# When the modulation blocks are multiplied, and where the decays' logarithms stand

## The chip, the cores and the metric

The kernel runs on one core of one Trainium2 chip. The metric is the device time of one execution in microseconds (us): lower is better. TensorE is called PE, VectorE DVE, ScalarE ACT, GpSimd POOL and SyncE SP; SP issues most of the transfers (DMA).

## The reference, cut to what matters

Two layers of a diffusion backbone over 512 latent tokens and 256 context tokens, width 1024. The first layer is a bidirectional retention with 4 heads, the second a gated MLP. Ahead of each layer the normed tokens are scaled and shifted by vectors that come from a conditioning vector (the modulation):

```python
shift_x, scale_x, gate_x = jnp.split(silu_c @ ada_w[i] + ada_b[i], 3, axis=-1)
shift_c, scale_c, gate_c = jnp.split(silu_cc @ ada_w[i] + ada_b[i], 3, axis=-1)
hx = rmsnorm(x, norm_g[i]) * (1 + scale_x[:, None]) + shift_x[:, None]
hc = rmsnorm(ctx, norm_g[i]) * (1 + scale_c) + shift_c
...
log_g = jax.nn.log_sigmoid(decay_logit.astype(F32))
...
q = to_heads(h @ w_in[:, :a], RET_HEADS)
k = to_heads(h @ w_in[:, a:bq], RET_HEADS) * (RET_QK_DIM ** -0.5)
v = to_heads(h @ w_in[:, bq:cq], RET_HEADS)
z = h @ w_in[:, cq:]
```

`log_g`, eight numbers (four heads, two directions), enters the retention as exponents of the decay between tokens.

## The kernel before, in words

The large products are done in single precision by splitting each operand into a high and a low part: three products (low by high, high by low, high by high) in place of one (`mm3`). ACT copies the high part and DVE subtracts it to get the low part (`split`, tiles `hl`). The token-times-weight products are further arranged as fast 2x2 block products with seven in place of eight (`Product`, with the names B11, T1, T2, B21, T3, B22, T4); the sums of blocks that this needs are formed by DVE, of the weights in the tiles `raw`, of the tokens in `oS1` to `oS4`, and of the results in the tiles `snap`. In a product 24 PE instructions belong to one step.

The first projection (`kq` of head 0) is plain, because its tokens are only just being made. It runs over eight blocks of 128 features, `kb` = 0 to 7; we call them steps. For each block:

- `ada0_mm(kb, ...)` multiplies the conditioning vector by the block's modulation weights (tile `ada_w`), 16 PE instructions per block, into one PSUM bank; ACT copies the bank to a tile `adae`.
- `ada0_cols(kb, es, n)` turns this by transposes, two per block, and four small DVE operations make the scale `gs0` and the shift `sh0` of the block, or of two blocks (n = 2).
- `come(...)` applies scale and shift to the block's tokens (DVE, ACT, DVE) and leaves the high and low part in tiles `oA..` and `oS..` (latent) or `hc` (context).
- `plain(kb, th, ...)` does the products of the block.

The context tokens come later: their two halves are loaded to `cq[0]` and `cq[1]`, transposed for their norms in `half_rows` after step 3, and `spread(2)` with the copy to `rs2` makes their norm factors after step 4. They enter in steps 4 to 6 (`CTX_COME`) and are multiplied in steps 5 to 7 (`CTX_PLAIN`).

Behind the first projection comes a pair of `vz` quads (values and gates of head 0, `PAIRED`), whose products alternate between the two quads, and then nine single quads (`SINGLE`), n = 0 to 8. Each is a stretch of about 24 us on PE. `decay_logs` makes `lg` from the eight logits in ten DVE operations and two of ACT (Exp and Ln) on tiles of 8 columns; before, it is called in the paired quads, after product B22 of the first quad. `lg` is first read by `decay(0)`, during n = 5.

What sets the order: each engine runs its instructions in the order in which they stand in its queue. Up to the end of the first projection this is the order of the text, for PE throughout. After that (`act.kept = dve.kept = False`) the instructions of ACT and DVE are put in order when the kernel is compiled, by what is ready, near the order of the text. SP issues loads in the order of the text; the weights `raw` go through a queue `Q` of loads and splits, and `Q.get()` hands out a split weight and sees that the next two are split as well. Small products of `ones` (`between_modes`) are put at chosen places in the stream of PE.

Of the kernel before, what the change touches and what calls it, by code (L numbers as in the profile page):

```python
# [67 lines left out]
def hybrid_kernel(ctx, tc, xT_d, cT_d, cv_d, sv_d, rows_d, ada0_d, adag_d, w_d, rope_d, dec_d, ws_d, id_d, out_d):  # L68
# [13 lines left out]
    def st(shape, tag, dt=F32, bufs=1, name=None):  # L82
        return sb.tile(shape, dt, tag=tag, name=name or tag, bufs=bufs)

    T2 = 11
# [32 lines left out]
    def t2(name, shape=(P, 512), dt=F32):  # L118
        return st(list(shape), "t2", dt, bufs=T2, name=name)

    def pt(shape=(P, 512), tag="ps"):
        return ps.tile(list(shape), F32, tag=tag, name="pst", bufs=6 if tag == "ps" else 2)
# [208 lines left out]
    def op(key):  # L331
        A[key] = st([P, 2, 4, HS], "o" + key, F32R)
# [12 lines left out]
    def features(bank, a, w, fresh, ks=range(4)):  # L345

        for kt in ks:
            if kt == 3 and inside:
                inside.pop(0)()
            r = (a[:, 0, kt, :], a[:, 1, kt, :])  # L350
            for s in range(2):
                o = s * 512 + kt * P
                mm3(bank[:, s * HS:s * HS + HS], (w[:, 0, o:o + P], w[:, 1, o:o + P]), r, fresh and kt == 0 and s == 0, kt == 3)
# [143 lines left out]
    def decay_logs():  # L497
        la = st([P, 8], "la")
        lb = st([P, 8], "lb")
        lc = st([P, 8], "lc")  # L500
        dve.tensor_scalar(la, dlog, -1.0, None, ALU.mult)
        dve.tensor_tensor(la, la, dlog, ALU.min)
        act.activation(la, la, AF.Exp)
        dve.tensor_scalar(lb, la, 1.0, None, ALU.add)
        act.activation(lg, lb, AF.Ln)
        dve.tensor_scalar(lc, lb, -1.0, None, ALU.add)
        dve.tensor_tensor(lc, la, lc, ALU.subtract)
        dve.reciprocal(lb, lb)
        dve.tensor_tensor(lc, lc, lb, ALU.mult)
        dve.tensor_tensor(lg, lg, lc, ALU.add)  # L510
        dve.tensor_scalar(la, dlog, 0.0, None, ALU.min)
        dve.tensor_tensor(lg, la, lg, ALU.subtract)
# [9 lines left out]
    def half_rows(at, g, t, tag="ps"):  # L522

        for i in range(2):
            pq = pt(tag=tag)
            for k in range(4):
                pe.transpose(pq[:, k * P:k * P + P], at(k)[:, i * P:i * P + P], ident)
            if i == 0:
                act.activation(t2("junk0"), pq, AF.Square, scale=1.0 / 32.0, accum_out=sq[t][:, g, 0:1])
            else:  # L530
                dve.bn_stats(bnx[:, t, g, :], pq)
# [23 lines left out]
    def ada0_mm(*kbs, then=None):  # L555

        n = len(kbs)
        pa = pt((P, HS * n), tag="tm")
        for i, kb in enumerate(kbs):
            rows = ada_w.pop(kb)  # L560
            for k in range(KT):
                j = k % 4
                mm(pa[32 * j:32 * j + 32, i * HS:i * HS + HS], cpad[:, k, :], rows[k // 4][:, j * HS:j * HS + HS],
                   start=(k < 4 and i == 0), stop=(k >= 4), skip_group_check=True)
        if then:
            then()
        e = t2("adae", (P, HS * n))
        act.copy(e, pa)
        return e

    def ada0_cols(k0, e, n=1):
        pq = pt((P, HS * n), tag="tm")
        for b in range(2 * n):
            pe.transpose(pq[:, b * P:b * P + P], e[:, b * P:b * P + P], ident)
        s = st([P, 2 * n, 2], "ada_s" if n == 1 else "ada_s2", bufs=2, name="ada_s")
        v = pq.rearrange("p (c g r) -> p c r g", c=2 * n, g=4)
        dve.tensor_reduce(s, v[:, :, 0:2, :], axis=AX.X, op=ALU.add)
        ss = s.rearrange("p (n b) r -> p n b r", b=2)
        ks = slice(k0, k0 + n)
        dve.tensor_tensor(gs0[:, ks, :], ss[:, :, 0, :], adab0[:, 1, ks, :], ALU.add)  # L580
        dve.tensor_tensor(sh0[:, ks, :], ss[:, :, 1, :], adab0[:, 0, ks, :], ALU.add)
        dve.scalar_tensor_tensor(gs0[:, ks, :], gs0[:, ks, :], 1.0, g0[:, ks, :], ALU.add, ALU.mult)
# [67 lines left out]
    def come(*what, then=None):  # L650


        made = []
        for kb, th in what:
            g, k = divmod(kb, 4)
            r = th // 2
            if r:
                f, h, l = cq[g][:, k, :], hc[:, 0, kb, :], hc[:, 1, kb, :]
            else:
                name = NAMES[th][g]  # L660
                if k == 0:
                    A[name] = st([P, 2, 4, HS], AT_S3.get(name, "o" + name), F32R)
                f, h, l = xk(th, g, k), A[name][:, 0, k, :], A[name][:, 1, k, :]
            dve.scalar_tensor_tensor(f, f, gs0[:, kb, r:r + 1], rs[th], ALU.mult, ALU.mult)
            made.append((f, sh0[:, kb, r:r + 1], h, l))
        if then:
            then()
        for f, b, h, l in made:
            act.activation(h, f, AF.Identity, bias=b, scale=1.0)
        for f, b, h, l in made:  # L670
            dve.scalar_tensor_tensor(l, f, b, f32(h), ALU.add, ALU.subtract)
# [3 lines left out]
    def plain(kb, th, nhs=range(2), product=None):  # L675

        g = kb // 4
        for nh in nhs:
            if th == 0 and kb % 4 == 0:
                w0[g, nh] = Q.get(ahead=0)  # L680
        if th == 2:
            if kb == 0:
                bank["c"] = pt()
            features(bank["c"], hc[:, :, 4 * g:4 * g + 4, :], w0[g, 0], g == 0, (kb % 4,))
            return
        for nh in nhs:
            if kb == 0:
                bank[th, nh] = pt()
            if product:
                product(bank[th, nh], A[NAMES[th][g]], w0[g, nh], g == 0, kb % 4)  # L690
            else:
                features(bank[th, nh], A[NAMES[th][g]], w0[g, nh], g == 0, (kb % 4,))
# [23 lines left out]
    es = ada0_mm(0)  # L716
# [8 lines left out]
    es = ada0_mm(1, then=lambda: come((0, 1)))  # L725
# [8 lines left out]
    es = ada0_mm(2)  # L734
# [15 lines left out]
    cut(w12, 2, 4)()  # L750
    plain(1, 0, (1,))
    plain(1, 1, (1,))
    es = ada0_mm(3, 4)
    shb = st([P, 4], "shb")
    plain_done = kq_done(0)
    held = {}
# [15 lines left out]
    for kb in range(2, 8):  # L772
        if kb == 3:
            Q.upto(3)
        plain(kb, 0, (0,))
        if kb in (2, 4, 6):
            ada0_cols(kb + 1, es, 1 if kb == 6 else 2)
        plain(kb, 0, (1,))
        if kb + 1 < 8:
            come((kb + 1, 0), (kb + 1, 1))  # L780
        if kb in (3, 7):
            Q.upto({3: 4, 7: 6}[kb])
        plain(kb, 1)
        if kb == 3:
            es = ada0_mm(5, 6)
            half_rows(lambda k: cq[0][:, k, :], 0, 2)
            half_rows(lambda k: cq[1][:, k, :], 1, 2, "tm")
            inverse(2)
        if kb == 4:
            es = ada0_mm(7)  # L790
        if kb == 2:
            Q.cap = None
            Q.pump()
        if kb == 4:
            rs[2] = copied(spread(2), "rs2")
        come(*((k, 2) for k in CTX_COME.get(kb, ())))
        if kb == 6:
            Q.upto(5)
        if kb == 7:
            hold((0, 0), (0, 1), (1, 0), (1, 1))  # L800
            op("S1")
            for x, y in zip(f21, f22):
                dve.tensor_tensor(y, x, y, ALU.add)
            dve.tensor_tensor(shb, sh0[:, 0:4, 0], sh0[:, 4:8, 0], ALU.add)
            for k in range(4):
                shifted(xk(1, 1, k), shb[:, k:k + 1], A["S1"][:, 0, k, :], A["S1"][:, 1, k, :])
        for k in CTX_PLAIN.get(kb, ()):
            plain(k, 2)
# [206 lines left out]
            pass  # L1015

    two = {q: project(q) for q in pair}
    sums = {("B11", 1): sum_s2, ("T1", 0): sum_s4, ("T2", 0): sum_s3, ("B22", 0): decay_logs}
    inside_t.append(between_modes)
    for name in PAIRED:  # L1020
        for i, q in enumerate(pair):
# [9 lines left out]
    for n, q in enumerate(QUADS[3:]):  # L1031
        pr = project(q)
        if n in (0, 3, 6, 8):
            inside_t.append(between_modes)
        if n == 5:
            inside.append(between_modes)
        for i, name in enumerate(SINGLE):
            pr.run(name, Q.get())
            if i % 2:
                popped()  # L1040
            if 2 not in pieces and i not in (2, 4):
                pieces.append(step())
            if n == 5 and i % 2 == 0:
                aside(dec0)
            if n == 8 or (n == 6 and i < 3):
                aside(qk0)
            if n == 8:
                aside(v0)
# [153 lines left out]
    sums = [st([P, 2, 2], f"sum{hf}", name="sums") for hf in range(2)]  # L1202
# [432 lines left out]
```

## Time and profile before

| what | before |
|---|---|
| time, median of 3 runs | 872.15 us (872.02 to 873.51) |
| profiled execution: time | 872.66 us |
| profiled execution: span | 870.5 us |
| PE busy | 860.2 us, 99% |
| DVE busy | 713.9 us, 82% |
| ACT busy | 457.9 us, 53% |
| read from memory | 128.58 MB |

The span is the time between the first and the last instruction in the trace; the execution's own time is 2.2 us longer. A row of a timeline gives the start in us, the length in us, the engine, the line, the operation, the tile written and those read, how many instructions were put together, and in brackets the idle time before them and what ended it. A row of the waits gives the total in us, the count and the longest. PEld is the load of the stationary operand into PE.

### The profile page before, as it was taken

How to read it: one execution, taken by the hardware profiler on the slowest of the kernel's cores; microseconds unless marked ns; L12 is line 12 of the kernel's file. 1: busy time of each engine (PE TensorE's matmuls, PEld its weight loads, DVE VectorE, ACT ScalarE, POOL GpSimd, SP SyncE). 2: the span in 40 equal slices, each digit the busy share in tenths (PEclk: the TensorE clock that was granted, in tenths of full speed). 3: DMA queues.
4: the chain of work that ended last, by engine and by line, in shares of the span. 5: the costliest groups of instructions: out<-in, count | busy, mean ns of one | idle time of the engine just before them, and what ended most of it. 6: DMA issues, size and time to landing. Idle time of an engine off the chain costs nothing.

```text
span 870.5 us, 16995 instructions
## 1 busy us (share of the span) xinstructions
PE 860.2 (99%) x6898; PEld 823.1 (95%) x6898; DVE 713.9 (82%) x1004; ACT 457.9 (53%) x711; POOL 58.4 (7%) x96
## 2 busy tenths in 40 slices
PE   8999999999999999999999999999999999999997
PEld 6799999999999999999989899999999899899986
DVE  4699978699789777888677679999899488688995
ACT  5475644434545346637364549744666456255434
POOL 0001201102102011000000002011000000000110
PEclk9999999999999999999999999999999999999999
DMA  9942968557577458747264602635436036035533
GB/s 360 403 144 94 332 208 269 160 180 236 197 237 242 146 193 322 271 153 248 72 200 163 205 13 104 201 133 206 135 122 194 25 122 199 20 122 170 121 42 106
DMA packets 74238, 153.81 MB, mean 177 GB/s; under 512 B 7728, under 2 KB 32816, under 8 KB 74160
## 3 DMA queue, kind: packets, MB, share of 16 engines
q1 hardware_dynamic: 65856, 128.40, 45.1%
q0 software_dynamic: 7872, 24.12, 8.4%
q8 instruction: 54, 0.88, 0.4%
q10 hardware_dynamic: 432, 0.20, 0.1%
q14 instruction: 24, 0.20, 0.1%
HBM read 128.58 MB, written 24.12 MB: 175 GB/s over the span
## 4 chain that ended last, share of the span: by engine, by line
PE 89%; DVE 6%; DMA 3%; ACT 1%; issue 1%; SPq 0%; DVEq 0%; ACTq 0%
PE pst L54 89%; DMA ada_w<-in_ada_dram 2%; DVE hl L54 2%; DVE raw L54 1%; DMA xs<-in_xT_dram 1%; DVE xs L54 1%; DVE oS L54 1%; DVE rope_a L54 0%; DVE o L54 0%; DVE snap L54 0%; DVE cq L54 0%; DVE hc L54 0%; ACT junk L54 0%; DVE rope_b L54 0%; DVE oA L54 0%
## 5 line engine op out<-in xcount | busy, mean ns | idle before, releaser
L54 DVE TENSOR_TENSOR hl<-raw,hl 128x1024 fp32r<-128x1024 f32 (+2 forms) x197 | 235.0, 1198 | 69.2 <-ACT hl L54 69.0
L54 ACT CAST hl<-raw 128x1024 fp32r<-128x1024 f32 (+2 forms) x197 | 202.8, 1034 | 137.1 <-DVE raw L54 58.6
L54 PE MATMUL pst<-hl,oS 128*128 128x256 f32 x1152 | 133.3, 276 | 0.0
L54 PE MATMUL pst<-oS,hl 128*128 128x256 f32 x1104 | 132.6, 277 | 0.0
L54 PEld LDWEIGHTS pst<-hl,oS 128*128 128x128 f32 x1152 | 131.8, 188 | 0.4 <-issue 0.4
L54 PEld LDWEIGHTS pst<-oS,hl 128*128 128x128 f32 x1104 | 128.2, 188 | 0.8 <-issue 0.8
L54 PE MATMUL pst<-oA,hl 128*128 128x256 f32 x936 | 116.5, 279 | 0.0
L54 PEld LDWEIGHTS pst<-oA,hl 128*128 128x128 f32 x936 | 110.6, 188 | 2.2 <-issue 0.8
L54 DVE TENSOR_TENSOR raw<-raw 128x1024 f32<-128x1024 f32 x92 | 111.8, 1218 | 0.8
L54 ACT COPY snap<-pst 128x512 f32<-128x512 f32 x92 | 53.6, 584 | 90.1 <-PE pst L54 90.0
L54 PE MATMUL pst<-hl,oA 128*128 128x256 f32 x768 | 92.8, 278 | 0.3 <-DVE snap L54 0.3
L54 PE MATMUL pst<-og,hl 128*128 128x256 f32 x768 | 91.1, 278 | 0.0
L54 PEld LDWEIGHTS pst<-hl,oA 128*128 128x128 f32 x768 | 89.7, 188 | 0.5 <-issue 0.5
L54 PEld LDWEIGHTS pst<-og,hl 128*128 128x128 f32 x768 | 89.2, 188 | 0.3
L54 PE MATMUL pst<-v,ph 128*128 128x512 f32 x192 | 59.8, 393 | 0.0
L54 PE MATMUL pst<-hl,ya 128*128 128x512 f32 (+1 forms) x246 | 59.1, 386 | 0.0
L54 PEld LDWEIGHTS pst<-hl,ya 128*128 128x128 f32 x246 | 45.3, 188 | 9.5
L54 DVE TENSOR_TENSOR snap<-pst,snap 128x512 f32<-128x512 f32 x69 | 47.2, 684 | 5.1 <-PE pst L54 5.1
L54 PE MATMUL pst<-hl,hc 128*128 128x256 f32 x384 | 46.1, 276 | 0.0
L54 PEld LDWEIGHTS pst<-hl,hc 128*128 128x128 f32 x384 | 44.7, 188 | 0.0
L54 ACT CAST ph<-pf 128x512 fp32r<-128x512 f32 x24 | 14.8, 618 | 55.2 <-DVE pf L54 52.8
L54 PEld LDWEIGHTS pst<-v,ph 128*128 128x128 f32 x192 | 36.1, 188 | 7.1
(186 smaller groups left out, 1021.2 us busy)
## 6 DMA issues: line engine op xcount, KB each, us to landing
raw<-in_w_dram SPq DMA_DIRECT2D x224, 256.0 KB, 3.9
bg<-in_adag_dram SPq DMA_DIRECT2D x32, 512.0 KB, 4.3
ada_w<-in_ada_dram SPq DMA_DIRECT2D x16, 512.0 KB, 8.7
raw<-in_w_dram SPq DMA_DIRECT2D x16, 512.0 KB, 4.3
bg<-in_dec_dram SPq DMA_DIRECT2D x12, 512.0 KB, 4.9
v<-snap POOLq DMA_DIRECT2D x16, 256.0 KB, 5.2
z<-snap POOLq DMA_DIRECT2D x16, 256.0 KB, 4.9
v<-v SPq DMA_DIRECT2D x8, 512.0 KB, 4.0
```

The costliest lines, as they stand in the source:

```text
L54: made = op(*args, **kw)
```

## The change: three modulation groups cut anew, and a call moved

Before, the modulation blocks are multiplied as 0, 1, 2, (3, 4), (5, 6), 7; after, as 0, 1, 2, 3, (4, 5), (6, 7). The group (4, 5) is multiplied at the end of step 2 and (6, 7) at the end of step 4, and their columns are turned in steps 3 and 5. The number of products and transposes is the same. The call of `decay_logs` moves from the paired quads to the second single quad (n = 1), after its third product T2.

```diff
-    es = ada0_mm(3, 4)
+    es = ada0_mm(3)
...
         plain(kb, 0, (0,))
-        if kb in (2, 4, 6):
-            ada0_cols(kb + 1, es, 1 if kb == 6 else 2)
+        if kb in (2, 3, 5):
+            ada0_cols(kb + 1, es, 1 if kb == 2 else 2)
         plain(kb, 0, (1,))
...
         plain(kb, 1)
+        if kb in (2, 4):
+            es = ada0_mm(kb + 2, kb + 3)
         if kb == 3:
-            es = ada0_mm(5, 6)
             half_rows(lambda k: cq[0][:, k, :], 0, 2)
             half_rows(lambda k: cq[1][:, k, :], 1, 2, "tm")
             inverse(2)
-        if kb == 4:
-            es = ada0_mm(7)
...
-    sums = {("B11", 1): sum_s2, ("T1", 0): sum_s4, ("T2", 0): sum_s3, ("B22", 0): decay_logs}
+    sums = {("B11", 1): sum_s2, ("T1", 0): sum_s4, ("T2", 0): sum_s3}
...
             pr.run(name, Q.get())
+            if (n, i) == (1, 2):
+                decay_logs()
```

## The prediction, written before the result was known

> **What bounds the kernel now.** I read the page first, then the waits of TensorE (PE), then the chain of waits in order of time, then the timelines of the places that these name.
>
> ```profile
> PE 860.2 (99%) x6898; PEld 823.1 (95%) x6898; DVE 713.9 (82%) x1004; ACT 457.9 (53%) x711; POOL 58.4 (7%) x96
> PEclk9999999999999999999999999999999999999999
> ```
> ```profile
> PE pst L54 <- DMA ada_w<-in_ada_dram: 0.9, 2, 0.6
> ...
> PE pst L54 <- DVE snap L54: 0.3, 1, 0.3
> ```
> ```profile
> 15.93 10.21 DMA ada_w<-in_ada_dram
> ...
> 100.23 758.87 PE pst L54 x6000
> ```
> The first fence is the page: PE is busy 99% of the span, at a granted clock of 0.9 or more in every slice. The second is what PE waited for up to 110 us, the third the chain. From 100.23 us to the tail the chain is 758.87 us of PE work and nothing else. So a microsecond won elsewhere counts only if it reaches PE before that point, and a delay of PE that is not won back by then ends in the total. The change touches both waits of the second fence: the modulation block whose weights came late (before 27 us), and VectorE (DVE) being late at 100 us. I take them in turn.
>
> **The modulation blocks.** Two rows of the weight-load timeline, and the issue and the landing of the second context half:
>
> ```profile
> 26.18 0.16 PEld L54 LDWEIGHTS pst<-ada_w,cpad 128*32 128x32 f32 x8 [1.08 <-DMA ada_w<-in_ada_dram]
> ...
> 36.35 0.85 PEld L54 LDWEIGHTS pst<-ident,cq 128*128 128x128 f32 x8 [0.35 <-PE pst L54]
> ```
> ```profile
> 28.65 0.33 SPq L54 DMA_DIRECT2D cq<-in_cT_dram  x1
> ```
> ```profile
> cq<-in_cT_dram SPq DMA_DIRECT2D x1, 512.0 KB, 7.6
> ```
> The last eight products of block 4 wait 1.08 us for their weights. With block 3 alone there, that wait goes: blocks 4 and 5 are multiplied one step (24 products) later, and should block 5 come late for that, PE waits ahead of 36.35, where it has time. But PE cannot keep this lead. The context transposes need the second half of the context, issued at 28.65 us and landed 7.6 us later, at 36.25 us; they start at 36.35 us. The releaser in brackets is PE itself, which had long issued its work; the landing time says that the wait is for the DMA. None of the loads up to there is issued later or earlier by this change: they stand before it in SP's order, in the same sequence and with the same bytes. So 36.35 us stays, PE only arrives earlier and waits longer: earlier by one block (0.94, half of the 1.87 below) and up to the 1.08, so 1.3 to 2.4 us in place of 0.35. What counts is the work that stands behind 36.35 us:
>
> ```profile
> 33.28 1.93 PE L54 MATMUL pst<-ada_w,cpad 128*32 128x256 f32 x32
> 35.15 2.30 PE L54 MATMUL pst<-ident,cq 128*128 128x128 f32 x16
> ...
> 38.00 0.60 PE L54 MATMUL pst<-ident,adae 128*128 128x128 f32 x4
> 38.36 2.30 PE L54 MATMUL pst<-oA,hl 128*128 128x256 f32 x18
> 40.58 1.07 PE L54 MATMUL pst<-ada_w,cpad 128*32 128x256 f32 x16
> 41.59 0.71 PE L54 MATMUL pst<-ident,sq 128*128 128x128 f32 x4
> ...
> 47.60 0.38 PE L54 MATMUL pst<-ident,adae 128*128 128x128 f32 x2
> 47.73 2.30 PE L54 MATMUL pst<-oA,hl 128*128 128x256 f32 x18
> ```
> Before, blocks 5 and 6 (33.28 to 35.15, 1.87 us) are done ahead of 36.35, and only block 7 (40.58 to 41.59, 1.01 us) lies behind it. After, 6 and 7 are one group behind it: 1.87 in place of 1.01, +0.86 us. The turned columns behind it were four transposes (5, 6) and two (7); now only four (6, 7), so the two go: from 47.60 to 47.73, and the product after them starts about 0.09 late, 0.22 us in all. Net +0.64 us on PE, with nothing to cover it, since PE is never idle between there and 100 us.
>
> Two small terms lie beside it. The transposes at 38.00 are also where the products fall into their faster pace (see below); without them 18 products may go slow, 18 x 4.2 ns = 0.08 us. And DVE:
>
> ```profile
> 46.18 0.89 DVE L54 SCALAR_TENSOR_TENSOR oA<-xs,sh,oA 128x256 fp32r<-128x256 f32 x2 [0.18 <-ACT oA L54]
> ```
> The first of these two is done near 46.66 us, halfway, and the six products of step 6 that read it stand ahead of the transposes of 47.60, so they start at 47.60 - 6 x 0.113 = 46.92: 0.26 us of room. After, four small DVE operations on the columns of 6 and 7 (0.16 each by the row at 84.23 below, 0.6 us) stand ahead of this step rather than behind it, and DVE's work on the context starts up to 0.4 us later (0.86, less 0.45 for the four transposes that no longer stand ahead of it). PE comes 0.64 and two transposes, 0.86, later. The room shrinks by at most 0.14 and stays; I take nothing, and 0.2 us as the other end.
>
> **The logarithms.** Rows of DVE and of ScalarE (ACT) in the paired quads:
>
> ```profile
> 84.23 0.16 DVE L54 TENSOR_SCALAR la<-sv 128x8 f32<-128x8 f32 x1
> 84.30 1.22 DVE L54 TENSOR_TENSOR raw<-raw 128x1024 f32<-128x1024 f32 x1
> ...
> 88.92 0.16 DVE L54 TENSOR_SCALAR lb<-la 128x8 f32<-128x8 f32 x1
> ...
> 89.61 1.23 DVE L54 TENSOR_TENSOR hl<-raw,hl 128x1024 fp32r<-128x1024 f32 x1
> ```
> ```profile
> 85.21 1.28 ACT L54 ACT_TABLE_LOAD   x1
> ...
> 88.41 1.28 ACT L54 ACT_TABLE_LOAD   x1
> 89.71 0.21 ACT L54 ACTIVATE lg<-lb 128x8 f32<-128x8 f32 x1
> ```
> ```profile
> 56.00:99.66 43.66, 43.66 (x387) 43.66 (x386) 42.98 (x69) 29.60 (x43) 6.29 (x10) 1.00 0.47 152
> ...
> 130.80:155.31 24.51, 24.51 (x219) 24.51 (x217) 20.67 (x20) 11.00 (x15) 3.40 (x5) 1.00 0.73 244
> ```
> In the windows table (columns PE, PEld, DVE, ACT, POOL) DVE is busy 42.98 of 43.66 us up to the wait: it runs back to back and loses ground. Ten small operations of the logarithms lie in it. A single one takes 0.07 us of its time (84.23 to 84.30), the four that stand together 0.69 (88.92 to 89.61). Six single at 0.07 to 0.11 and 0.69 make about 1.2 us that DVE gets back before 100 us. What that is worth on PE:
>
> ```profile
> 78.02 21.92 PE L54 MATMUL pst<-hl,oS 128*128 128x256 f32 x192
> 100.23 6.71 PE L54 MATMUL pst<-hl,oA 128*128 128x256 f32 x54 [0.29 <-DVE snap L54]
> 106.78 0.38 PE L54 MATMUL pst<-ones 128*128 128x128 f32 x2
> ```
> ```profile
> 128.10 5.60 PE L54 MATMUL pst<-hl,oA 128*128 128x256 f32 x48
> 133.54 2.88 PE L54 MATMUL pst<-hl,hc 128*128 128x256 f32 x24
> ...
> 155.31 2.99 PE L54 MATMUL pst<-oA,hl 128*128 128x256 f32 x24
> 158.13 2.05 PE L54 MATMUL pst<-hc,hl 128*128 128x256 f32 x16
> ```
> Start to start, the products have two paces: 48 in 5.44 us (113.3 ns) at 128.10, and 24 in 2.82 us (117.5 ns, 4.2 ns more) at 155.31, after the two operands change sides. At 78.02 it is the fast one: 192 would take 21.76 us, but the next group starts 22.21 us later. The wait thus costs 0.45 us with the restart, not only the 0.29 shown. Behind it the 54 products up to the "ones" products take 6.55 us, where the fast pace takes 6.12: 0.43 more. From there to 128.10 the next 186 products and the two "ones" take 21.32 us, the fast pace again. Without the wait both go: -0.88 us. The sum that PE waits for was written just before 100.23; after, DVE comes to it 1.2 us earlier and up to 0.4 later, near 99.4, while PE wants it at 78.02 + 21.76 + 0.64 = 100.4. There is a microsecond of room, so I take the whole 0.88; the ends are 0 and 0.88.
>
> In the second single quad (130.80 to 155.31, this is n = 1) DVE has 24.51 - 20.67 = 3.8 us free and ACT 13.5. The ten operations (1.2 us) and three table loads (Exp, Ln and back to Silu, 3 x 1.28 = 3.84 us of ACT) fit in. Weights are split two products ahead, 5.4 us, which is the cover; if it were gone, PE would wait a load or two, 1.3 to 2.6 us. I take nothing.
>
> The Trainium skill ("ScalarE: Activation LUTs", "What ACT_TABLE_LOAD costs") says that a load is followed by a drain of about 1.38 us, 2.66 us for each switch. By that the three would hold ACT 8 us; the sum stays as it is, since 13.5 are free, and the row behind 88.41 shows Ln starting 0.02 us after the load's end.
>
> **The sum.** +0.86 - 0.22 + 0.08 + 0 - 0.88 = -0.16 us. The profiled execution took 872.66 us (span 870.5), so it would take 872.5; it lies 0.5 over the median of the three runs, 872.15, and on that the forecast is 872.0. Within 0.2% (1.7 us, about what a measurement of this kernel can tell from no change) that is no change: one wait is removed, the other only moved to the transfer after it.
>
> **The rivals.**
>
> *Slower: a short wait early in the paired quads.* At the start of the window of 56.00 us stand such "ones" products too, and the fast pace held from there to 100 us; the wait at 100.23 shows that one wait loses it until the next such products. If PE, in its new place against DVE and ACT, met a wait of 0.2 us soon after, the products up to 100 us (the window above counts 387) would go at 117.5 ns: 387 x 4.2 ns = 1.63. With the 0.64 above, the 0.2, and only 0.45 of the 0.88 won: +2.0 us, 874.2. It decides from a wait within the first 60 products or so. Against it: PE comes later there than DVE does, so the room grows. For it: small differences decide the pace, and DVE has no idle time to recover. 15%.
>
> *Slower: the logarithms stall the second single quad.* One table load not covered, 1.3 us, the slow pace to 155.31 (at most 0.5), with +0.64 and -0.88: +1.6; with two loads +2.9, 875.0. Against: the free time above. 5%.
>
> *Slower: the clock.* PE now idles 1.3 to 2.4 us before 36.35, with transposes alone around it.
>
> ```profile
> 6.63 2.16 PE L54 MATMUL pst<-ident,xs 128*128 128x128 f32 x18 [1.69 <-DMA ident<-in_id_dram]
> ```
> An idle stretch of 1.69 us with transposes behind it stands here too, and the clock line showed no drop. If it dropped all the same for the 24 products of step 4, they would take twice 113.3 ns: +2.7, with the rest +2.6, 874.7. The Trainium skill ("TensorE: Matmul & The Clock Gate", "Why this matters for your kernels") puts the limit at idle gaps of more than about 3 us; by that rule the clock holds, unless transposes do not count as work, and the row above speaks against that. 4%.
>
> *No gain at 100 us.* DVE's order changes and the wait there stays: +0.64 to +1.2, 872.8 to 873.4, no change. 9%.
>
> *Faster: 36.35 does not bind.* Were that wait PE's own, as the bracket says, the 1.08 us won at 26 us would stay and nothing would be deferred: -1.08 - 0.88 = -1.96, 870.2. Against: the landing at 36.25. 8%. That the compiler puts the instructions in another order without loss leaves 4% for faster.
>
> **How the numbers follow.** The forecast gets 55%, with its own range of 871.2 to 873.2. No change: 55 + 9 = 64%. Slower: 15 + 5 + 4 = 24%. Faster: 8 + 4 = 12%. The range from 870.9 to 874.3 takes in the forecast, the lost gain and the first slower rival, and leaves out the two rarer slower ones and the faster one, 17%.
>
> **What would show it.** Right: PE no longer waits for ada_w at 26 us; context transposes of the second half still start at 36.3 to 36.4, after more than 1 us of idle time; the transposes of 41.59 come 0.2 to 0.6 us later; no wait for snap at 100 us, and 113 ns there; the table loads stand between 138 and 152 us. Wrong: the second context half landing at another time, a PE wait between 57 and 100 us, or 117 ns over tens of microseconds.

## The result, and the profile after

| | before | after |
|---|---|---|
| median | 872.28 us (871.94 to 873.51, 22 runs) | 873.58 us (872.98 to 875.24, 22 runs) |
| profiled execution | 872.66 us, span 870.5 | 874.63 us, span 872.4 |

The ratio is 1.0016, 95% interval 1.0009 to 1.0022: the kernel became slower by about 1.3 us. That is less than 0.2%, but with 22 runs of each the measurement tells it from no change; 872.0 was forecast. What PE waited for in the whole span after:

```profile
PE pst L54 <- DMA ident<-in_id_dram: 2.0, 1, 2.0
PE pst L54 <- DVE eps L54: 1.1, 1, 1.1
PE pst L54 <- DVE snap L54: 0.9, 1, 0.9
PE pst L54 <- DVE hl L54: 0.9, 1, 0.9
```
The wait for `ada_w` is gone, as meant. The wait for `snap` at 100 us is not gone but three times as long, and a new one for `hl` has come. The weight-load timeline has the new one in step 4:

```profile
34.71 0.90 PEld L54 LDWEIGHTS pst<-ident,cq 128*128 128x128 f32 x8
35.84 0.86 PEld L54 LDWEIGHTS pst<-ident,cq 128*128 128x128 f32 x8 [0.23 <-issue]
36.66 0.77 PEld L54 LDWEIGHTS pst<-oA,hl 128*128 128x128 f32 x6
38.56 2.19 PEld L54 LDWEIGHTS pst<-oA,hl 128*128 128x128 f32 x18 [1.12 <-DVE hl L54]
40.87 1.45 PEld L54 LDWEIGHTS pst<-ada_w,cpad 128*32 128x32 f32 x32
42.74 0.52 PEld L54 LDWEIGHTS pst<-ident,sq 128*128 128x128 f32 x4 [0.41 <-PE pst L54]
```
PE comes early to the context transposes (34.71), waits there for the second half, and starts it at 35.84. Six products later it stands for 1.12 us. ACT and DVE show why (ACT's timeline, then DVE's):

```profile
31.56 0.59 ACT L54 COPY adae<-pst 128x512 f32<-128x512 f32 x1 [2.13 <-PE pst L54]
32.04 1.05 ACT L54 CAST hl<-raw 128x1024 fp32r<-128x1024 f32 x1
35.40 0.91 ACT L54 ACTIVATE oA<-xs,sh 128x256 fp32r<-128x256 f32 x2 [2.31 <-DVE xs L54]
36.21 1.03 ACT L54 CAST hl<-raw 128x1024 fp32r<-128x1024 f32 x1
```
```profile
33.12 1.23 DVE L54 TENSOR_TENSOR hl<-raw,hl 128x1024 fp32r<-128x1024 f32 x1 [3.18 <-ACT hl L54]
...
34.88 0.88 DVE L54 SCALAR_TENSOR_TENSOR xs<-xs,gs,rs 128x256 f32<-128x256 f32 x2
...
37.28 1.23 DVE L54 TENSOR_TENSOR hl<-raw,hl 128x1024 fp32r<-128x1024 f32 x1 [0.45 <-ACT hl L54]
```
In ACT's queue the copy of the columns of blocks 4 and 5 (31.56) now stands ahead of the cast of weight B21 (32.04), and it waits 2.13 us for PE. DVE has nothing to do for 3.18 us, because its own next instruction is the low part of that weight. Then everything that follows in the two queues is late: the scaling for step 4 at 34.88, behind it the cast of weight B22 at 36.21, its low part from 37.28 to 38.5, and PE, which needs it, at 38.56.

The length of this wait is not the change's doing alone. In the opening of this execution the 32 transposes of the latent tokens went slowly (PE's timeline after, then the windows from 8 to 10 us after and before; columns length, PE, PEld, DVE, ACT, POOL, granted clock, DMA share, GB/s):

```profile
6.89 5.35 PE L54 MATMUL pst<-ident,xs 128*128 128x128 f32 x32 [1.97 <-DMA ident<-in_id_dram]
```
```profile
8.00:10.00 2.00, 2.00 (x11) 2.00 (x10) 0.70 (x1) 0.94 (x4) 0.00 (x0) 0.50 1.04 420
```
```profile
8.00:10.00 2.00, 1.80 (x17) 1.57 (x15) 1.24 (x3) 1.23 (x4) 0.00 (x0) 1.00 1.04 420
```
The granted clock was 0.50 there, and 1.00 before. A transpose took up to 421 ns, where before has 273 in the middle, and PE is more than a microsecond late from then on: it has the products of blocks 4 and 5 at 29.55, where a kernel with the same opening (the mended one, below) has them at 28.23 in an execution whose transposes were not slow. The low part of B22 ends 8.96 us after these products start (29.55 to 38.51). An estimate from these numbers: from 28.23 on it would end near 37.2, before the 37.75 at which PE had its first six products of step 4 behind it in that execution (36.98, and the 0.77 that the six take above), and PE would not have waited. By this estimate it takes both, the copy's new place and a late PE, to make the wait; no second execution of the change was traced. The transposes took as long in the executions of two other kernels (modulation part alone, logarithms really moved; 421 ns in the middle), although the clock recorded there is 1.00. The second of these opens like before, so the slow opening does not come from the change.

At 100 us (PE's timeline, and DVE's further up):

```profile
102.24 6.38 PE L54 MATMUL pst<-hl,oA 128*128 128x256 f32 x54 [0.93 <-DVE snap L54]
108.47 0.38 PE L54 MATMUL pst<-ones 128*128 128x128 f32 x2
```
```profile
88.80 0.17 DVE L54 TENSOR_SCALAR la<-sv 128x8 f32<-128x8 f32 x1
89.00 0.17 DVE L54 TENSOR_TENSOR la<-la,sv 128x8 f32<-128x8 f32 x1
89.08 1.22 DVE L54 TENSOR_TENSOR hl<-raw,hl 128x1024 fp32r<-128x1024 f32 x1
90.22 0.16 DVE L54 TENSOR_SCALAR lb<-la 128x8 f32<-128x8 f32 x1
...
90.83 0.17 DVE L54 TENSOR_SCALAR la<-sv 128x8 f32<-128x8 f32 x1
90.91 1.22 DVE L54 TENSOR_TENSOR hl<-raw,hl 128x1024 fp32r<-128x1024 f32 x1
...
106.15 0.16 DVE L54 TENSOR_TENSOR lc<-lc,lb 128x8 f32<-128x8 f32 x1
```
The logarithms did not follow their call. It stands some 50 us further down in the text, but the order of DVE and ACT is made when the kernel is compiled, out of what is ready, and their input had been there from the start. So most of them still stand among the paired quads, from 88.80 where before has 84.23; only the last ones slid behind 100 us.

### The profile page after: what moved, and what is told of

The parts are those of the page before. It is cut to its first block, busy times and chain, and to the rows that moved or that the text cites. A ratio compares the mean times of both kernels' runs of the same rounds, so it can differ in the third digit from the quotient of the medians.

```text
span 872.4 us, 16998 instructions
## 1 busy us (share of the span) xinstructions
PE 861.6 (99%) x6898; PEld 825.1 (95%) x6898; DVE 713.5 (82%) x1004; ACT 458.0 (52%) x711; POOL 58.6 (7%) x96
## 4 chain that ended last, share of the span: by engine, by line
PE 87%; DVE 6%; DMA 3%; ACT 1%; issue 1%; SPq 0%; DVEq 0%; ACTq 0%
PE pst L54 87%; DMA ada_w<-in_ada_dram 2%; DVE hl L54 2%; DVE raw L54 1%; DMA raw<-in_w_dram 1%; DMA xs<-in_xT_dram 1%; DVE xs L54 1%; DVE oS L54 1%; DVE rope_a L54 0%; ACT hl L54 0%; DVE o L54 0%; DVE cq L54 0%; DVE hc L54 0%; ACT junk L54 0%; DVE snap L54 0%
```

## The experiments

For each kernel the "ones" products that stood at 106.78 us before are a mark behind which PE waits for nothing. The last column is the mark less the start of the second context half's transposes (36.35 before), so that the moment at which the first transfers arrive, which differs between executions, drops out. In two kernels it does not drop out cleanly: in the change and in the modulation part alone PE restarts behind the wait for `hl`, at 38.56 and 38.47, when DVE lets it, so an early context only makes that wait longer, and the last column is an upper end. By the mark alone, which stands at 106.78, 106.36 and 106.19 in three executions of before, these two are 1.7 to 2.3 and 0.9 to 1.5 us behind.

| kernel | median, us | ratio to before (95%) | mark, us | mark less context, against before |
|---|---|---|---|---|
| the change | 873.58 | 1.0016 (1.0009 to 1.0022) | 108.47 | +2.20 |
| modulation part alone | 873.37 | 1.0013 (1.0004 to 1.0022) | 107.67 | +1.75 |
| logarithms moved in the text alone | 872.62 | 1.0003 (0.9994 to 1.0012) | 106.46 | +0.08 |
| logarithms really moved | 871.83 | 0.9997 (0.9988 to 1.0006) | 105.59 | -0.85 |
| modulation part, cast first | 872.95 | 1.0008 (0.9999 to 1.0016) | 107.06 | +0.36 |
| the change, both faults mended | 872.47 | 1.0002 (0.9993 to 1.0011) | 106.52 | -0.25 |
| block 6 ahead of the context | 872.22 | 1.0000 (0.9991 to 1.0008) | 105.45 | see below |
| mended, context loaded first | 871.71 | 0.9994 (0.9985 to 1.0002) | 105.10 | see below |

The first four experiments ran beside runs of before with a median of 872.32, the next three beside 872.16.

**The modulation part alone.** The call of `decay_logs` is back in the paired quads.

```diff
-    sums = {("B11", 1): sum_s2, ("T1", 0): sum_s4, ("T2", 0): sum_s3}
+    sums = {("B11", 1): sum_s2, ("T1", 0): sum_s4, ("T2", 0): sum_s3, ("B22", 0): decay_logs}
...
-            if (n, i) == (1, 2):
-                decay_logs()
```

> Only the modulation groups are changed; the logarithms stay where they were. Theory A (the whole loss comes from the modulation part: one more block behind the context transposes, and a DVE wait of about 1 us in step 4 because ACT's copy of the columns of 4 and 5 now stands ahead of the split of the weight B21): 1.2 to 2.0 us slower than before, with the PE wait for hl near 38 us. Theory B (the two parts share it, the call moved in the text disturbs the order in the paired quads): 0.6 to 0.8 us slower.

```profile
PE pst L54 <- DVE hl L54: 1.1, 1, 1.1
PE pst L54 <- DVE eps L54: 1.1, 1, 1.1
PE pst L54 <- DMA ident<-in_id_dram: 0.8, 1, 0.8
```
These are all the waits of PE in it. The new wait for `hl` is there and the one for `snap` is not: PE itself comes so late to 100 us that DVE is no longer behind. The time is 1.05 us over before (873.37 against 872.32), most of the 1.30 of the whole change. This is just under the range of theory A, and the interval (0.3 to 1.9 us) takes in that of B. In the traces the modulation part has at most 1.75 of the change's 2.20; the rest comes with the call, through the longer wait at 100 us. So most of the loss is the modulation part's, as in A, but the call has a share in the trace, as in B; neither holds as it stands.

**The call moved in the text alone.** The modulation groups of before, `decay_logs()` in the second single quad as in the change.

> Only the call of the logarithms is moved in the text. Theory A (the compiler puts most of them back among the paired quads, so DVE has about the same work before 100 us): within 0.3 us of before, PE's wait for snap at 100 us still there, the logarithms' operations between 84 and 107 us. Theory B: 0.5 us or more slower. What the prediction held (they leave the paired quads): 0.9 us faster.

```profile
PE pst L54 <- DVE snap L54: 0.7, 1, 0.7
```
```profile
87.21 0.17 DVE L54 TENSOR_SCALAR la<-sv 128x8 f32<-128x8 f32 x1
87.41 0.17 DVE L54 TENSOR_TENSOR la<-la,sv 128x8 f32<-128x8 f32 x1
...
97.67 0.69 DVE L54 TENSOR_TENSOR rope_a<-held,rope 128x512 f32<-128x512 f32 x1
99.41 0.69 DVE L54 TENSOR_TENSOR snap<-pst,snap 128x512 f32<-128x512 f32 x1
```
The first fence is the wait at 100 us among PE's waits, the second the first of the logarithms in DVE's timeline, and the sum that PE waits for (`snap`). Without the modulation part, too, they stay in the paired quads, and the median (+0.30) cannot be told from before: theory A. The wait is longer than before's 0.29, because the new order also lets an operation of the rope (97.67) pass ahead of the sum; before it stands behind the sum, at 100.00. PE's mark is hardly later, counted from the context (+0.08), because the 54 products behind the wait took 6.22 us, where before has 6.55. The 0.9 us that the prediction held is excluded.

**The logarithms really moved.** Their operations are tied to the ones before them in the text.

```diff
             if (n, i) == (1, 2):
+                act.pinned = dve.pinned = True
                 decay_logs()
+                act.pinned = dve.pinned = False
```

> The call is moved and its operations are tied to their place in the text, so that they really run in the second single quad; the modulation groups are those of before. Theory A: no PE wait at 100 us, the fast pace through it, 0.4 to 0.9 us faster than before. Rival (DVE's lateness at 100 us does not come from the 1.2 us of the logarithms, or the table loads stall the second single quad): no change or slower.

```profile
99.47 6.28 PE L54 MATMUL pst<-hl,oA 128*128 128x256 f32 x54
105.59 0.38 PE L54 MATMUL pst<-ones 128*128 128x128 f32 x2
```
```profile
139.65 0.16 DVE L54 TENSOR_SCALAR la<-sv 128x8 f32<-128x8 f32 x1
...
142.85 0.17 DVE L54 TENSOR_SCALAR lb<-la 128x8 f32<-128x8 f32 x1 [1.70 <-ACT la L54]
...
145.31 0.20 DVE L54 RECIPROCAL lb<-lb 128x8 f32<-128x8 f32 x1 [1.19 <-ACT lg L54]
```
No bracket at 99.47: the wait has gone, and the 54 products take 6.12 us, the fast pace. Counted from the context, PE is 0.85 us ahead at the mark. In the second single quad DVE waits twice for ACT's table loads, 1.70 and 1.19 us, and PE does not wait for it. The median is 0.49 us lower; its interval takes in both 0 and the 0.85, so the gain is shown in the trace and not in the time alone.

**The modulation part with the cast ahead.** `Q.upto(3)`, which splits weight B21, moves from the start of step 3 to ahead of the products of blocks 4 and 5.

```diff
-        if kb == 3:
-            Q.upto(3)
...
+        if kb == 2:
+            Q.upto(3)
         if kb in (2, 4):
             es = ada0_mm(kb + 2, kb + 3)
```

> As the modulation part alone, but the split of the weight B21 is put ahead of the products of blocks 4 and 5, so that ACT does it before the copy of their columns. Theory A: the PE wait for hl near 38 us goes, and only the later block is left: 0.5 to 0.9 us slower than before, 0.6 to 1.1 faster than the modulation part alone. Rival (the wait in step 4 is for the transfer of the weight, not for ACT's order): as slow as the modulation part alone.

```profile
33.92 0.89 PEld L54 LDWEIGHTS pst<-ident,cq 128*128 128x128 f32 x8
36.27 0.86 PEld L54 LDWEIGHTS pst<-ident,cq 128*128 128x128 f32 x8 [1.46 <-issue]
37.09 2.89 PEld L54 LDWEIGHTS pst<-oA,hl 128*128 128x128 f32 x24
40.12 1.45 PEld L54 LDWEIGHTS pst<-ada_w,cpad 128*32 128x32 f32 x32
```
```profile
PE pst L54 <- DMA cq<-in_cT_dram: 1.2, 1, 1.2
```
The 24 products of step 4 run through, 37.09 to 40.12: no wait for `hl`. This run alone does not show why. Its opening was not slow, and PE had the products of blocks 4 and 5 at 28.34, where the modulation part alone had them at 29.46; by the estimate above that could have done away with the wait too. The mended kernel below tells the two apart. The wait before the context transposes now bears the name that the prediction had to infer, the DMA of `cq`. The median is 0.63 us over before and 0.42 under the modulation part alone; in the trace the difference to that one is 1.4 us (the last column). The trace is that of theory A and the 0.63 lies in its range; the 0.42 lies under its 0.6 to 1.1.

**Both faults mended.** The change with the two edits above.

> The whole change with its two faults mended: the logarithms are tied to the second single quad, and the split of weight B21 stands ahead of the products of blocks 4 and 5. Theory A (later block +0.64, logarithms out of the paired quads -0.88, nothing else): 0.2 us faster than before, within 0.5 of it, and 1.2 to 1.8 faster than the change as it was made. Rival (something else in the change costs time, which the two faults only cover): 0.8 us or more slower than before.

This is the kernel that the prediction's sum was made for. In its first execution PE was as late as in the modulation part alone (products of blocks 4 and 5 at 29.42, because of a wait of 0.81 us for modulation weights at 21 us). ACT's rows, one of DVE and one of the weight loads:

```profile
29.95 1.05 ACT L54 CAST hl<-raw 128x1024 fp32r<-128x1024 f32 x1 [0.66 <-DMA raw<-in_w_dram]
31.42 0.59 ACT L54 COPY adae<-pst 128x512 f32<-128x512 f32 x1 [0.42 <-PE pst L54]
```
```profile
36.14 1.23 DVE L54 TENSOR_TENSOR hl<-raw,hl 128x1024 fp32r<-128x1024 f32 x1 [0.81 <-ACT hl L54]
```
```profile
37.16 2.82 PEld L54 LDWEIGHTS pst<-oA,hl 128*128 128x128 f32 x24
```
The copy stands at 31.42, as in the modulation part alone (31.46), but the cast of B21 is done before it, and the low part of B22 ends at 37.37 in place of 38.42. PE has no wait. In the modulation part alone PE wanted that weight at 37.14 (its 1.33 us of waiting ended at 38.47), because the context came earlier there; with the low part done at 37.37, 0.23 us would have been left. So, by this estimate, some 1.1 us of that wait was ACT's order.

Two more executions of it, and two more of before:

> The kernel before once more, for a look at two things that may differ between executions of one kernel: when the first weights land, and whether the products between 549 and 566 us go at the fast pace (113 ns) or the slow (118). Theory A (both are chance, not the change): the landing varies by 0.5 us, and the slow stretch turns up in some executions of either kernel. Rival (the slow stretch belongs to kernels whose order in the paired quads was changed): none in this kernel.

> A second look at the kernel before. Theory A (chance): landing and pace differ from the other look by up to 0.5 and 0.8 us. Rival: the same pace at 549 us in each look at this kernel, the fast one.

> The mended change once more. Theory A: PE is again 0.1 to 0.4 us ahead of before at 105 us, counted from the landing of the second context half, and the slow stretch at 549 us is there in some looks only. Rival: the slow stretch is there in every look at this kernel.

> A second look at the mended change. Theory A (chance): the pace at 549 us need not be that of the other looks. Rival: slow there in every look at this kernel, 0.7 to 0.8 us lost each time.

In three executions of the mended kernel the mark stands at 106.52, 106.33 and 106.39, and the transposes at 36.34, 36.15 and 36.15: 70.18, 70.18 and 70.24 us apart, where the three of before have 70.43, 70.42 and 70.29. So 0.05 to 0.25 us were gained, where the sum said 0.16. The median, +0.31 us, is at the slow edge of what was expected and agrees with any value from -0.6 to +1.0; it is 1.1 us under that of the change, just short of the 1.2 to 1.8 expected. Part of what blurs it is seen in one window of these executions (columns PE, PEld, DVE, ACT, POOL, then granted clock, DMA share and GB/s; first one of before, then two of the mended kernel):

```profile
548.60:566.00 17.40, 17.40 (x151) 17.40 (x149) 17.40 (x21) 12.92 (x17) 1.62 (x3) 1.00 0.74 234
```
```profile
548.60:566.00 17.40, 17.40 (x149) 17.40 (x148) 17.40 (x20) 12.71 (x17) 1.62 (x3) 1.00 0.74 231
```
```profile
548.60:566.00 17.40, 17.40 (x155) 17.40 (x155) 17.40 (x20) 13.46 (x17) 1.62 (x3) 1.00 0.74 236
```
The same stretch holds 149 products in one execution of the mended kernel and 155 in another, and ACT's work in it goes with that (12.71 and 13.46 us busy): 6 products in 155 are 4% of 17.4 us, some 0.7 us. Before has 151 in the execution shown, and 155 and 156 in its two others. So the slower pace belongs to neither kernel, and the rival, that it belongs to one of them, falls. From the mark to the end the three executions of before took 765.9, 766.0 and 766.5 us, and those of the mended kernel 766.8, 766.1 and 766.2, which is some 0.7 us from one to another within either kernel.

**Block 6 ahead of the context.** Logarithms held; blocks 3 | 4, 5 | 6 | 7, with 6 multiplied and turned in step 3, and the cast of B21 ahead as above.

```diff
-    es = ada0_mm(3, 4)
+    es = ada0_mm(3)
...
+        if kb == 3:
+            es = ada0_mm(6)
...
+        if kb == 2:
+            Q.upto(3)
+            es = ada0_mm(4, 5)
         if kb == 3:
-            es = ada0_mm(5, 6)
+            ada0_cols(6, es)
```

> Logarithms tied as above; blocks 3 | 4, 5 | 6 | 7, with 6 multiplied and its columns turned in step 3, ahead of the context transposes, and only 7 behind them. Theory A (only what stands behind the wait for the second context half counts): PE is 0.4 to 0.5 us ahead of before at 48 us (four transposes fewer behind the wait), and 1.0 to 1.4 us faster in all. Rival (the work of PE is the same, so its place does not matter): as the logarithms tied alone, 0.5 us faster than before.

```profile
PE pst L54 <- DVE ada_s L54: 0.4, 1, 0.4
```
PE is 1.33 us ahead of before at the mark, but the second half's transposes were early by 0.65 in this execution, and turning the columns there makes a wait of its own (above): the last four transposes wait for the bank that DVE still reads. The median does not differ from before, where 1.0 to 1.4 or 0.5 us less was expected. Neither theory is shown.

**The context loaded first.** The mended change, with both context halves loaded ahead of blocks 6 and 7.

```diff
     Q.pump_n(1)
-    ada0_load(6)
     load(cq[0], cT_d[:, 0:4, :])
     Q.pump_n(1)
     load(cq[1], cT_d[:, 4:8, :])
+    ada0_load(6)
     ada0_load(7)
```

> As the mended change, but the two context halves are loaded ahead of modulation blocks 6 and 7. Theory A (the transposes wait for the landing of the second half, and for nothing else): they start some 2 us earlier, no wait before them, and the kernel is 1.3 to 2.3 us faster than before. Rival (PE meets the weights of block 7 or the chain of DVE instead, and loses it again): within 0.4 us of the mended change.

```profile
33.97 1.77 PEld L54 LDWEIGHTS pst<-ident,cq 128*128 128x128 f32 x16
35.70 2.86 PEld L54 LDWEIGHTS pst<-oA,hl 128*128 128x128 f32 x24
38.69 1.45 PEld L54 LDWEIGHTS pst<-ada_w,cpad 128*32 128x32 f32 x32
```
All 16 transposes run in one piece from 33.97, with no wait between them. At the mark PE is 1.2 to 1.4 us ahead of the three executions of the mended kernel and 1.1 to 1.7 ahead of those of before. This is the lowest median of all, 871.71: 0.45 us under before, and 0.76 under the mended change. Its interval, 0.9985 to 1.0002, just takes in no change. The 0.45 lies under the range of theory A, and the 0.76 beyond that of the rival, so the times decide for neither. Some 0.5 us of its lead was given up in the profiled execution between 380 and 402 us, again at a slower pace and without a wait.

## Why the prediction was wrong, point by point

- *The wait for the second context half stays.* Right, but not in the change's own execution as described: 0.23 us of idle time there, not 1.3 to 2.4. PE had lost its lead in the slow opening, and the second half was issued at 28.08, where before has 28.65 (28.20 to 28.65 in its three executions). In the kernel with the cast first the wait bears the name of the transfer, and the idle time is 1.46; in the mended one it is 0.86, 1.50 and 1.38. Where PE is late and the context early, as with the modulation part alone, the wait is gone. The transposes of the second half start between 35.49 and 36.35, by the execution (leaving out the kernel that loads the context first).
- *One more block behind it: +0.64.* Right. In the mended kernel the long run of products that begins at 78.02 before begins at 78.64, 42.30 us after the second half's transposes; before it is 41.67: +0.63. In the kernel with the cast first the mark is at +0.36, which is this less some of the wait at 100 us that PE, coming later, no longer meets.
- *DVE's 0.26 us of room in step 6, "I take nothing".* The room held, but a step failed beside it: only DVE's small operations were followed. The prediction did not walk ACT's queue past the moved copy. In step 3 that copy now stands ahead of the cast of B21, and with PE late it put 1.12 us of waiting on PE in step 4. "What is queued behind the instruction that now waits" was the question to ask there, and it was asked only of PE.
- *The logarithms give DVE 1.2 us, PE 0.88.* The price on PE was right (0.85 when they really move), and so was the cover in the second single quad. DVE comes to the sum only 0.53 us earlier then, counted from the context, and not 1.2, because the rope operation passes ahead of it there too; it was enough. The step that failed is the plain one before it, that the moved call moves the work. The kernel's description on record says that order is made by what is ready; what is ready from the start need not follow the text. "No gain at 100 us" was among the rivals, at 9%, but without saying that the logarithms would stay, and without the longer wait, 0.93 in place of 0.29.
- *The sum.* With both faults mended the trace shows -0.05 to -0.25, where -0.16 was written. The terms of the sum held; two steps between text and queues did not. Of the 1.46 us between -0.16 and the measured +1.30, 0.88 is the gain that did not come; the remaining 0.6 is put down to the new wait for `hl` and the longer one at 100 us, which together cost more than that in the profiled execution.
- *The range.* The measured 873.58 lies inside 870.9 to 874.3, but by luck: the upper end stood for a short wait early in the paired quads, and none came.
- *The clock.* Where it was feared it held: after idle times of 0.9 to 1.5 us before the transposes the granted clock was 1.00 from 36.3 to 42 us. The rule of the Trainium skill ("TensorE: Matmul & The Clock Gate", "Why this matters for your kernels"), that only gaps of more than about 3 us count, agrees there. But it fell to 0.50 in the opening of the change's execution, after 1.97 us of idle time with transposes behind it, at the very place that the prediction took for its safe example (1.69 us before). By gaps alone the rule does not give that drop, and no run here shows why it came in this execution. The clock line of the page could not show it: its first digit, a mean over 22 us, is 9 in both kernels.
- *A stall in the second single quad.* None came, not even where the logarithms really ran there.

What stays open is how the traces and the medians fit together. The change is 1.7 to 2.3 us behind at the mark and 1.30 in the medians; the logarithms held are 0.85 ahead and 0.49 in the medians. The chance paces later in the kernel, and an opening that is slow in some executions only, are large enough for it, but their share in the timed runs was not seen, since these have no trace.

## What to carry to other kernels

Before pricing a moved instruction, find where it lands in the queue of its own engine: if a compiler orders that queue, what a call does can stay behind when the call is moved in the text, unless it is tied. Then ask of each instruction that will wait, here a small copy on ACT, what stands behind it in the same queue and whom that feeds. And a wait that ends with a transfer cannot be shortened by coming earlier; only the work that stands behind it, or the order of the transfers, counts. Last, trace a second execution before you explain a wait: here one was set by a late opening as much as by the change.

## What the hardware showed that was not expected

PE has two paces for the same stream of products, 113.3 and about 117.5 ns, and which one it takes after a wait is partly chance: the wait at 100.23 us before left it slow (54 products in 6.55, 6.54 and 6.42 us in three executions), the longer wait at 102.24 after did not, or not throughout (6.23 us for the 54 from 102.24 to 108.47, where the fast pace gives 6.12), and the stretch at 549 us took either in executions of one kernel. In a kernel that PE bounds this alone moves the time by some 0.7 us, by the estimate above. The granted clock fell to 0.50 for about 3 us in the opening of one execution, after 1.97 us of idle time, and did not in one of before, after 1.69. The first transfers, too, come up to half a microsecond apart between executions of the same code: the second context half's transposes start at 36.35, 35.94 and 35.90 in three executions of before.
